# SSD stage of a hybrid backbone: two buffers for the turned tiles, and chunk products, weighted x and the chunk output's reads at later places

## The chip, the cores and the metric

The kernel runs on one core of a Trainium2 chip. The metric is the device time of one execution in microseconds. Four engines compute: TensorE (PE; its weight loads are PEld), VectorE (DVE), ScalarE (ACT) and GpSimd (POOL). SyncE (SP) issues most transfers, in the order in which they stand in its queue; a transfer that has to wait keeps those behind it waiting.

## The reference

One layer of a trunk over 256 latent tokens with 256 context tokens ahead of them. A combined input projection feeds two groups of heads, a bidirectional Mamba-2 SSD and a spatial-gating MLP, whose outputs go through one output projection. What the change touches is the SSD, cut here to what matters:

```python
def _ssd(xh, dt, A, Bm, Cm, h0, with_output):
    # x (heads' values), B and C (state space), chunks of 128 tokens
    xdt = x * dtc[..., None]
    acs = jnp.cumsum(a, axis=2)
    decay_to_end = jnp.exp(a_tot[:, :, None] - acs)
    states = jnp.einsum('bckgn,bckgr,bckgrp->bcgrpn', Bc, decay_to_end, xdt)
    ...                                     # h_starts: states carried from chunk to chunk
    CB = jnp.einsum('bcqgn,bckgn->bcgqk', Cc, Bc)
    y_diag = jnp.einsum('bcgqk,bcgrqk,bckgrp->bcqgrp', CB, Lmat, xdt)
    y_off = jnp.einsum('bcqgn,bcgrpn,bcqgr->bcqgrp', Cc, h_starts, jnp.exp(acs))
    return (y_diag + y_off).reshape(bsz, L, H, P), final
```

It runs forward and backward over the latents, starting from the context's final states, for 8 groups of 4 heads. x, B and C come from the projection through a depthwise convolution of 5 taps and SiLU.

## The kernel before

All products of the projections are in three passes with split operands: each weight tile w is split into hi (ScalarE, line 543) and lo (VectorE, line 549), and TensorE multiplies hi by hi, lo by hi and hi by lo (lines 141 to 143). The SSD stage starts after the adaLN and the first seven tiles of the projection and takes the profile's span from about 126 to 450 us. In it TensorE streams the other 25 of 32 channel tiles through (psx); each has 48 such products (16 k-steps of three), 512 or 256 columns wide.

The tiles come in groups of four: tile 4g and 4g+1 are x of group g, 4g+2 is B, 4g+3 is C. Seven tiles, among them 12, 13 and 15 of group 3, are made early and only convolved in this stage. After a tile is done, its work on the other engines is put into a queue by due times: `later(dt, fn)` files a function, `pump(dt)`, which the loop calls after every second k-step (6 products) with 1.3 (0.65 for 256 columns), advances a counter of due time and calls what is due. So a due time fixes the place of each instruction in its engine's order, and each engine works its own order off, waiting on semaphores.

For a tile: `conv_tile` sets the first tap on ScalarE (out of the accumulator psx), the other taps on VectorE (line 624, eight instructions, four for a C tile) and SiLU on ScalarE (line 627). For a group:

- x and B have to be turned (channels by tokens to tokens by channels). `by_pe` says where TensorE does it (ptx, ptb, then a ScalarE copy): group 0, and B of group 7. Elsewhere `turn` has VectorE transpose 32x32 blocks into a buffer T (tag tt: tiles tx, tb; line 739), SyncE stores T to DRAM (a tile D: Dx, Db; line 741), and `turned` reads it back by four transfers of 64 KB (xk, bk; line 747). The time allowed between both is `LAND`, 4.5.
- `ssd_w` (GpSimd) weighs x by decay for context and latents: xw in four instructions, xl in two; `ssd_sk` writes the skip term into y in two.
- `ssd_cb`, `ssd_states` (TensorE): pcb = B by C, psc = turned B by xw, psl = turned B by xl. Then `ssd_hc` (ScalarE copies psc to hs), `ssd_hd` (GpSimd decays hs), `ssd_hl` (VectorE adds psl), `ssd_o` (TensorE, pso = C by hs).
- In between, `ssd_cbm`, `ssd_mb`, `ssd_m` make M and E from pcb and the decays for both chunks, `ssd_yd` multiplies E by x (psy). `ssd_yo` and `ssd_ya` scale pso (VectorE) and add it to y (GpSimd).
- `ssd_yc` turns psy through the same path (yc, Dy), `ssd_yt` reads it back (yz), `ssd_yf` adds it to y (VectorE, line 968).
- `row_load` (GpSimd's queue, line 725) loads R, the cumulated decays of the next group, after E was taken from the one before.

The weights' raw tiles (w, 1 MB each) are loaded three ahead by SyncE, in the same queue as the turned tiles.

Of the kernel before, what the change touches and what calls it, by code (L numbers as in the profile page):

```python
# [8 lines left out]
F32 = mybir.dt.float32  # L9
# [6 lines left out]
P = 128  # L16
# [4 lines left out]
NGRP = 8  # L21
# [26 lines left out]
def tile_hybrid_ssd_mlp(  # L48
# [22 lines left out]
    def mkpool(**kw):  # L71
        return tc.tile_pool(reuse_waits="tile", **kw)
# [23 lines left out]
    y = ypool.tile([P, 2, D], F32, tag="big16", name="y")  # L96
# [48 lines left out]
    def bc(ap, axis, n):  # L145
        u = ap.unsqueeze(axis)
        shp = list(u.shape)
        shp[axis] = n
        return u.to_broadcast(shp)
# [22 lines left out]
    def spt(shape, name):  # L172
        return sps.tile(shape, F32, tag="s", name=name)
# [162 lines left out]
    for k in range(KT):  # L336
# [7 lines left out]
        g = k % 4  # L344
# [169 lines left out]
    wp["spl"] = ctx.enter_context(mkpool(name="splp", bufs=4))  # L514
    cvs = ExitStack()
    drp = ctx.enter_context(mkpool(name="drp", bufs=1, space=bass.MemoryType.DRAM))
    drt = ctx.enter_context(mkpool(name="drt", bufs=2, space=bass.MemoryType.DRAM))
    cv1 = cvs.enter_context(mkpool(name="cv1", bufs=1))
    cv2 = cvs.enter_context(mkpool(name="cv2", bufs=2))
    cv3 = cvs.enter_context(mkpool(name="cv3", bufs=3))  # L520
# [57 lines left out]
    def later(dt, fn):  # L578
        queue.append((now[0] + dt, seq[0], fn))
        seq[0] += 1  # L580
# [14 lines left out]
    def conv_tile(i, src, d0, ds):  # L595
        ch = ORDER[i]
        lat = ch >= 24
        n = 256 if lat else 512
        cw = pc[:, C_CW + 5 * i : C_CW + 5 * i + 5]
        l0 = 0 if lat else 256  # L600
        T = {}

        def tap0():
            if ch < 16:
                o = cv3.tile([P, n], F32, tag="xs", name=f"xbc{i}")
            else:
                o = cv2.tile([P, n], F32, tag="cs" if lat else "bs", name=f"xbc{i}")
            nc.scalar.activation(o, src, AF.Identity, bias=pc[:, C_CB + i : C_CB + i + 1], scale=cw[:, 2:3])  # L608
            T["o"] = o

        def taps():
            o = T["o"]
            o4 = o[:, l0 : l0 + 256].rearrange("p (r t) -> p r t", r=4)
            src4 = src[:, l0 : l0 + 256].rearrange("p (r t) -> p r t", r=4)
            for k in (0, 1, 3, 4):
                s = k - 2
                parts = [(o4, src4, 64)]
                if not lat:
                    parts.append((o[:, 0:256], src[:, 0:256], 256))
                for (a, z, w) in parts:  # L620
                    o0, o1 = max(0, -s), w - max(0, s)
                    ao = a[..., o0:o1]
                    zi = z[..., o0 + s : o1 + s]
                    nc.vector.scalar_tensor_tensor(ao, zi, cw[:, k : k + 1], ao, op0=ALU.mult, op1=ALU.add)  # L624

        def silu():
            nc.scalar.activation(T["o"], T["o"], AF.Silu)
            done[i] = T["o"]

        later(d0, tap0)  # L630
        later(d0 + 0.9, taps)
        later(d0 + ds, silu)
# [12 lines left out]
    def wctx(t, d):  # L645
        return eu[:, 4 + t if d == 0 else t]

    def wlt(d):
        return eu[:, 3 - d]
# [80 lines left out]
    gs_ = {}  # L730
# [2 lines left out]
        return ap.rearrange("p (h q) -> p h q", h=4)  # L733

    def by_pe(g, what):
        return g == 0 or g == NGRP - 1 and what != "x"

    def turn(T, src, nm):
        nc.vector.transpose(T.rearrange("p (b g c) -> p g b c", b=4, g=4), src.rearrange("p (g b c) -> p g b c", g=4, b=4))
        D = drt.tile([64, 1024], F32, tag="D", name=f"D{nm}")  # L740
        nc.sync.dma_start(D.rearrange("(b g a) (i c) -> (a i) (b g) c", b=4, g=4, c=32),
                            T.rearrange("p (u c) -> p u c", c=32))
        return D

    def turned(dst, D):
        for b in range(4):
            nc.sync.dma_start(dst[32 * b : 32 * b + 32].rearrange("p (u c) -> p u c", c=32),
                                D[16 * b : 16 * b + 16, :].rearrange("u (i c) -> i u c", c=32))

    def ssd_x(g, xi):  # L750
        S = gs_.setdefault(g, {})
        if xi == 0:
            S["xk"] = cv2.tile([P, 2, 4, P], F32, tag="xk", name=f"xk{g}")
        xt = done.pop(4 * g + xi)
        if not by_pe(g, "x"):
            T = cv1.tile([P, 512], F32, tag="tt", name=f"tx{g}{xi}")
            S["Dx", xi] = turn(T, xt, f"x{g}{xi}")
            return
        p = spt([P, 4, P], f"ptx{g}{xi}")
        for t in range(4):  # L760
            nc.tensor.transpose(p[:, t, :], xt[:, t * P : (t + 1) * P], ident)
        S["ptx", xi] = p

    def ssd_xc(g, xi):
        xk = gs_[g]["xk"][:, xi]
        if by_pe(g, "x"):
            nc.scalar.copy(xk, gs_[g]["ptx", xi])
        else:
            turned(xk.rearrange("p t c -> p (t c)"), gs_[g]["Dx", xi])

    def xtok_(g, t):
        return gs_[g]["xk"][:, :, t].rearrange("p x (h q) -> p x h q", h=2)

    def hx(ap):
        return ap.rearrange("p (x h q) -> p x h q", x=2, h=2)

    def hb(ap):
        return bc(ap.rearrange("p (x h) -> p x h", x=2), 3, 64)

    def ssd_w(g):  # L780
        S = gs_[g]
        h4 = slice(4 * g, 4 * g + 4)
        xw = cv1.tile([P, 2, 2, 256], F32, tag="xw", name=f"xw{g}")
        for t in range(2):
            for d in range(2):
                nc.gpsimd.tensor_tensor(hx(xw[:, t, d, :]), xtok_(g, t), hb(wctx(t, d)[:, h4]), op=ALU.mult)
        xl = cv1.tile([P, 2, 256], F32, tag="xl", name=f"xl{g}")
        for d in range(2):
            nc.gpsimd.tensor_tensor(hx(xl[:, d, :]), xtok_(g, 2 + d), hb(wlt(d)[:, h4]), op=ALU.mult)
        S["xw"], S["xl"] = xw, xl  # L790

    def ssd_b(g):
        bt = done[4 * g + 2]
        S = gs_.setdefault(g, {})
        S["bk"] = cv1.tile([P, 4, P], F32, tag="bk", name=f"bk{g}")
        if not by_pe(g, "b"):
            T = cv1.tile([P, 512], F32, tag="tt", name=f"tb{g}")
            S["Db"] = turn(T, bt, f"b{g}")
            return
        p = spt([P, 4, P], f"ptb{g}")  # L800
        for t in range(4):
            nc.tensor.transpose(p[:, t, :], bt[:, t * P : (t + 1) * P], ident)
        S["ptb"] = p
# [101 lines left out]
    def yg(g, c):  # L905
        return y[:, c, g * 256 : (g + 1) * 256]

    def ssd_sk(g):
        for c in range(2):
            nc.gpsimd.tensor_tensor(hx(yg(g, c)), xtok_(g, 2 + c), hb(dsk[:, 4 * g : 4 * g + 4]), op=ALU.mult)  # L910
# [59 lines left out]
    LAND = 4.5  # L970

    def plan_tile(i, src, d0=0.0, ds=5.2, tx=7.0, tw=1.5, late=0.0, td=0.0):

        g, r = divmod(i, 4)
        conv_tile(i, src, d0, ds)
        lx, lb, ly = (0.7 if by_pe(g, w) else LAND for w in "xby")
        if lx == LAND:
            tw = max(tw, 2 * LAND + 3)
        if lb == LAND:
            late = max(late, 8.0)  # L980
        if r < 2:
            later(d0 + tx, lambda: ssd_x(g, r))
            later(d0 + tx + lx, lambda: ssd_xc(g, r))
        if r == 1:
            later(d0 + tx + tw, lambda: ssd_w(g))
            later(d0 + tx + tw + 3, lambda: ssd_sk(g))
        if r == 2:
            later(d0 + tx, lambda: ssd_b(g))
            later(d0 + tx + lb, lambda: ssd_bc(g))
        if r == 3:  # L990
            d0 += late
            for t, fn in [(6, ssd_cb), (6, ssd_states), (6.9, ssd_cbm), (7.6, lambda g: ssd_mb(g, 0)), (8, ssd_hc),
                          (8.7, ssd_hd), (9.4, ssd_hl), (9.5, lambda g: ssd_m(g, 0)), (11.2, lambda g: ssd_mb(g, 1)),
                          (12, ssd_o), (12.2, lambda g: ssd_m(g, 1)), (13.9, lambda g: ssd_yo(g, 0)),
                          (14.5, lambda g: ssd_yo(g, 1)), (14.7, lambda g: ssd_ya(g, 0)), (15.3, lambda g: ssd_ya(g, 1)),
                          (16 + td, ssd_yd), (16.9 + td, ssd_yc),
                          (16.9 + td + (1.7 if ly < 1 else LAND), ssd_yt), (18.6 + td + (0.7 if ly < 1 else 2 * LAND + 2), ssd_yf)]:
                later(d0 + t, lambda fn=fn: fn(g))
            plan_d(d0 + 11, g + 1, 1.5)
            plan_e(d0 + 17, g + 1)  # L1000
# [17 lines left out]
    for n, i in enumerate(REST):  # L1018
        lat = ORDER[i] >= 24
        ps = acp.tile([P, 256 if lat else 512], F32, tag="acc", name=f"psx{i}")  # L1020
        for hf in range(2):
            whi, wlo = half(2 * n + hf)
            for kk in range(8):
                k = 8 * hf + kk
                w = slice(kk * P, (kk + 1) * P)
# [167 lines left out]
    for blk in range(16):  # L1193
# [11 lines left out]
        for u in range(8):  # L1205
            whi, wlo = half(base + blk * 8 + u)
            for kk in range(2):
                k = 2 * u + kk
                w = slice(kk * 512, (kk + 1) * 512)
# [69 lines left out]
    for i in range(8):  # L1279
        tk, b = divmod(i, 4)  # L1280
# [156 lines left out]
```

## Time and profile before

| what | us |
|---|---|
| median of 3 runs | 978.4 (976.14 to 978.86) |
| the profiled execution | 974.69 |
| its span, first to last instruction | 972.8 |
| TensorE busy in the span | 955.7 |
| VectorE busy | 685.6 |
| GpSimd busy | 198.6 |

A line of the page's groups gives the source line, engine, operation, out<-in, the count, the busy us and mean ns, and the idle time in front. A line of waits gives the engine and what it waited for, then us in total, times and the longest. In the chain of waits and the timeline the first figure is the start in us from the span's start, the second the length. A line of a stretch gives its bounds and length, then each engine's busy us with its instructions (PE, PEld, DVE, ACT, POOL), TensorE's granted clock, the share of the DMA engines and GB/s. A name ending in q is an engine's queue of issues.

### The profile page before, as it was taken

What the parts mean: (1) busy time and instruction counts of PE and PEld (TensorE: products, weight loads), DVE (VectorE), ACT (ScalarE), POOL (GpSimd) and SP (SyncE); (2) the same over time, 40 slices, a digit from 0 to 9 for tenths busy, and PEclk for the clock granted to TensorE, in tenths of its full rate; (3) what the DMA queues carried; (4) which work ended last, traced back from release to release, by engine and by line L of the source; (5) the groups of instructions that cost most, each with busy time, mean ns of one, the idle gap of its engine ahead of it and who ended that gap; (6) DMA issues with size and microseconds to landing.
All of it is one profiled execution on the core that took longest, in us unless ns stands there. A gap on an engine that the chain in (4) does not pass through costs nothing.

```text
span 972.8 us, 13786 instructions
## 1 busy us (share of the span) xinstructions
PE 955.7 (98%) x5138; PEld 771.8 (79%) x5138; DVE 685.6 (70%) x1101; ACT 482.8 (50%) x731; POOL 198.6 (20%) x290
## 2 busy tenths in 40 slices
PE   9999999998997999999999999999999999999997
PEld 4688888786785878787888888887888888888885
DVE  6888798878985868676767776767666665445636
ACT  4344458564662544455445433465565564346612
POOL 0000002522551233354000000043334541000000
PEclk9999999999999999999999999999999999999999
DMA  9999956567676666575877868686556665556722
GB/s 363 417 415 415 365 224 165 149 182 158 138 189 169 147 172 149 160 217 209 295 304 281 289 254 314 259 305 210 200 195 222 223 233 192 212 177 251 266 87 86
DMA packets 145666, 225.09 MB, mean 231 GB/s; under 512 B 114992, under 2 KB 115248, under 8 KB 122944
## 3 DMA queue, kind: packets, MB, share of 16 engines
q1 hardware_dynamic: 138816, 206.55, 62.6%
q0 software_dynamic: 6208, 16.85, 5.4%
q8 instruction: 40, 0.66, 0.3%
q10 hardware_dynamic: 576, 0.82, 0.2%
q14 instruction: 26, 0.21, 0.1%
HBM read 211.02 MB, written 8.98 MB: 226 GB/s over the span
## 4 chain that ended last, share of the span: by engine, by line
PE 87%; DMA 6%; DVE 4%; ACT 1%; SPq 1%; issue 1%; DVEq 0%; ACTq 0%
PE pa L1212 12%; PE pa L1214 12%; PE pa L1213 12%; PE psx L141 8%; PE psx L142 8%; PE psx L143 8%; PE pm L1255 3%; PE pm L1254 3%; PE pm L1253 3%; DMA ada<-in_wada_dram 3%; PE pq L1255 2%; PE pq L1254 2%; PE pq L1253 2%; PE psc L865 2%; PE pso L917 1%; DMA wst<-in_wst_dram 1%
## 5 line engine op out<-in xcount | busy, mean ns | idle before, releaser
L88 DVE TENSOR_TENSOR lo_w<-w,hi_w 128x1024 fp32r<-128x1024 f32 x173 | 210.7, 1222 | 148.8 <-ACT hi_w L87 148.7
L87 ACT CAST hi_w<-w 128x1024 fp32r<-128x1024 f32 x173 | 182.2, 1053 | 220.7 <-PE pa L1214 147.9
L1212 PE MATMUL pa<-hi_w,hhi 128*128 128x512 f32 x512 | 201.2, 393 | 0.0
L1213 PE MATMUL pa<-lo_w,hhi 128*128 128x512 f32 x512 | 199.4, 390 | 0.0
L1214 PE MATMUL pa<-hi_w,hlo 128*128 128x512 f32 x512 | 199.4, 389 | 0.0
L141 PE MATMUL psx<-hhi,hi_w 128*128 128x512 f32 (+1 forms) x400 | 151.5, 379 | 0.0
L143 PE MATMUL psx<-hhi,lo_w 128*128 128x512 f32 (+1 forms) x400 | 145.8, 364 | 0.0
L142 PE MATMUL psx<-hlo,hi_w 128*128 128x512 f32 (+1 forms) x400 | 145.7, 364 | 0.0
L1212 PEld LDWEIGHTS pa<-hi_w,hhi 128*128 128x128 f32 x512 | 96.2, 188 | 20.9 <-issue 1.6
L1214 PEld LDWEIGHTS pa<-hi_w,hlo 128*128 128x128 f32 x512 | 96.1, 188 | 20.0
L1213 PEld LDWEIGHTS pa<-lo_w,hhi 128*128 128x128 f32 x512 | 96.2, 188 | 19.8 <-issue 0.2
L624 DVE SCALAR_TENSOR_TENSOR xbc<-psx,pc,xbc 128x248 f32<-128x248 f32 (+1 forms) x204 | 83.4, 473 | 19.7 <-ACT xbc L608 19.0
L549 DVE TENSOR_TENSOR lo_w<-w,hi_w 128x1024 fp32r<-128x1024 f32 x61 | 81.8, 1349 | 20.0 <-ACT hi_w L543 20.0
L1120 POOL DMA_DIRECT2D Z<-T x128 | 73.7, 583 | 97.2 <-ACT sq L1188 33.0
L141 PEld LDWEIGHTS psx<-hhi,hi_w 128*128 128x128 f32 x400 | 75.5, 189 | 14.4 <-issue 3.1
L142 PEld LDWEIGHTS psx<-hlo,hi_w 128*128 128x128 f32 x400 | 75.6, 189 | 12.9 <-issue 1.7
L143 PEld LDWEIGHTS psx<-hhi,lo_w 128*128 128x128 f32 x400 | 75.5, 189 | 12.2
L543 ACT CAST hi_w<-w 128x1024 fp32r<-128x1024 f32 x61 | 63.6, 1045 | 42.5 <-PE psx L142 29.5
L1253 PE MATMUL pm<-hi_w,hhi 128*128 128x512 f32 x128 | 49.8, 389 | 0.0
L1255 PE MATMUL pm<-hi_w,hlo 128*128 128x512 f32 x128 | 49.8, 389 | 0.0
L1254 PE MATMUL pm<-lo_w,hhi 128*128 128x512 f32 x128 | 49.8, 389 | 0.0
L378 ACT CAST hi_st<-wst 128x448 fp32r<-128x448 f32 (+2 forms) x26 | 17.2, 679 | 57.0 <-DMA wst<-in_wst_dram 57.0
(274 smaller groups left out, 1407.6 us busy)
## 6 DMA issues: line engine op xcount, KB each, us to landing
w<-in_wlat_dram SPq DMA_DIRECT2D x64, 1024.0 KB, 4.8
w<-in_wout_dram SPq DMA_DIRECT2D x32, 1024.0 KB, 4.8
w<-in_wxbc_dram SPq DMA_DIRECT2D x25, 1024.0 KB, 5.6
ada<-in_wada_dram SPq DMA_DIRECT2D x24, 1024.0 KB, 14.0
gate<-in_wada_dram SPq DMA_DIRECT2D x16, 1024.0 KB, 5.0
ada<-in_wada_dram SPq DMA_DIRECT2D x16, 512.0 KB, 12.5
R<-acs POOLq DMA_DIRECT2D x8, 1024.0 KB, 7.0
wst<-in_wst_dram SPq DMA_DIRECT2D x15, 480.0 KB, 13.0
```

The costliest lines, as they stand in the source:

```text
L87: nc.scalar.copy(hi, raw)
L88: nc.vector.tensor_tensor(lo, raw, hi.bitcast(F32), op=ALU.subtract)
L141: nc.tensor.matmul(ps, lhsT=whi, rhs=hhi[k][:, s], start=start, stop=False)
L142: nc.tensor.matmul(ps, lhsT=whi, rhs=hlo[k][:, s], start=False, stop=False)
L143: nc.tensor.matmul(ps, lhsT=wlo, rhs=hhi[k][:, s], start=False, stop=stop)
L624: nc.vector.scalar_tensor_tensor(ao, zi, cw[:, k : k + 1], ao, op0=ALU.mult, op1=ALU.add)
L1212: nc.tensor.matmul(pa[tk], lhsT=hhi[k][:, t], rhs=whi[:, w], start=k == 0, stop=False)
L1213: nc.tensor.matmul(pa[tk], lhsT=hhi[k][:, t], rhs=wlo[:, w], start=False, stop=False)
L1214: nc.tensor.matmul(pa[tk], lhsT=hlo[k][:, t], rhs=whi[:, w], start=False, stop=k == KT - 1)
L1253: nc.tensor.matmul(p, lhsT=yh[:, t], rhs=whi[:, w], start=j == 0, stop=False)
L1254: nc.tensor.matmul(p, lhsT=yh[:, t], rhs=wlo[:, w], start=False, stop=False)
L1255: nc.tensor.matmul(p, lhsT=yl[:, t], rhs=whi[:, w], start=False, stop=hf == 0 and j == 15)
```

## The change

It has five parts. The turning buffer tt has two copies instead of one, and the DRAM tiles four instead of two. In group 7 the second x tile (tile 29) is turned by TensorE instead of VectorE and DRAM. `ssd_w` is cut in two: xl becomes `ssd_wl`, due 3 later where x is turned through DRAM, and the skip is due another 3 later. The group's products with B and all that follows them (`late`) are due 11 instead of 8 after the C tile, 14 with tile 15 (it was 10). The reads of the turned chunk output are due 3 later and their addition to y 4 later.

```diff
-    drt = ctx.enter_context(mkpool(name="drt", bufs=2, space=bass.MemoryType.DRAM))
+    drt = ctx.enter_context(mkpool(name="drt", bufs=4, space=bass.MemoryType.DRAM))
...
     def by_pe(g, what):
-        return g == 0 or g == NGRP - 1 and what != "x"
+        return g == 0 or g == NGRP - 1 and what != "x0"
...
-        if not by_pe(g, "x"):
-            T = cv1.tile([P, 512], F32, tag="tt", name=f"tx{g}{xi}")
+        if not by_pe(g, f"x{xi}"):
+            T = cv2.tile([P, 512], F32, tag="tt", name=f"tx{g}{xi}")
...
+        S["xw"] = xw
+
+    def ssd_wl(g):
+        h4 = slice(4 * g, 4 * g + 4)
         xl = cv1.tile([P, 2, 256], F32, tag="xl", name=f"xl{g}")
         for d in range(2):
             nc.gpsimd.tensor_tensor(hx(xl[:, d, :]), xtok_(g, 2 + d), hb(wlt(d)[:, h4]), op=ALU.mult)
-        S["xw"], S["xl"] = xw, xl
+        gs_[g]["xl"] = xl
...
-            T = cv1.tile([P, 512], F32, tag="tt", name=f"tb{g}")
+            T = cv2.tile([P, 512], F32, tag="tt", name=f"tb{g}")
...
-        lx, lb, ly = (0.7 if by_pe(g, w) else LAND for w in "xby")
+        lx, lb, ly = (0.7 if by_pe(g, w) else LAND for w in (f"x{r}", "b", "y"))
...
         if lb == LAND:
-            late = max(late, 8.0)
+            late = max(late, 14.0 if i == 15 else 11.0)
...
         if r == 1:
+            late_w = lx == LAND
             later(d0 + tx + tw, lambda: ssd_w(g))
-            later(d0 + tx + tw + 3, lambda: ssd_sk(g))
+            later(d0 + tx + tw + (3 if late_w else 0), lambda: ssd_wl(g))
+            later(d0 + tx + tw + (6 if late_w else 3), lambda: ssd_sk(g))
...
-                          (16.9 + td + (1.7 if ly < 1 else LAND), ssd_yt), (18.6 + td + (0.7 if ly < 1 else 2 * LAND + 2), ssd_yf)]:
+                          (16.9 + td + (1.7 if ly < 1 else LAND + 3), ssd_yt), (18.6 + td + (0.7 if ly < 1 else 2 * LAND + 6), ssd_yf)]:
```

How this moves instructions shows in three places. The first is SyncE around group 4's B: bk4 is read from Db4, which holds tb4; yz3 is the chunk output of group 3, read from Dy3; w17 and w18 are weights. Before:

```order
L747 DMA xk4_2733<-Dx41_2855 32x16x32 x4
L741 DMA Dy3_2975<-yc3_2973 128x16x32
L741 DMA Db4_3024<-tb4_3022 128x16x32
L81 DMA w17_3058<-in_wxbc_dram 128x2048
L747 DMA yz3_3032<-Dy3_2975 32x16x32 x4
L747 DMA bk4_3021<-Db4_3024 32x16x32 x4
L81 DMA w18_3150<-in_wxbc_dram 128x2048
```

Now:

```order
L747 DMA xk4_2714<-Dx41_2829 32x16x32 x4
L741 DMA Db4_3014<-tb4_3012 128x16x32
L741 DMA Dy3_3018<-yc3_3016 128x16x32
L81 DMA w17_3050<-in_wxbc_dram 128x2048
L747 DMA bk4_3011<-Db4_3014 32x16x32 x4
L747 DMA yz3_3083<-Dy3_3018 32x16x32 x4
L81 DMA w18_3134<-in_wxbc_dram 128x2048
```

B's store and reads have each changed places with the chunk output's.

The second is TensorE at group 4's products with B, among the products of tile 21; the number behind hhi and hlo is the k-step. Before:

```order
L142 MATMUL psx21_3088<-hlo5_137,hi_w28_2956 128x512
L143 MATMUL psx21_3088<-hhi5_121,lo_w28_2985 128x512
L848 MATMUL pcb4_3122<-xbc19_3004,xbc18_2896 128x128 x2
L865 MATMUL psc4_3125<-xw4_3037,bk4_3021 128x512 x2
L868 MATMUL psl4_3128<-xl4_3042,bk4_3021 128x256 x2
L141 MATMUL psx21_3088<-hhi6_122,hi_w28_2956 128x512
```

Now:

```order
L142 MATMUL psx21_3088<-hlo11_143,hi_w29_2978 128x512
L143 MATMUL psx21_3088<-hhi11_127,lo_w29_3000 128x512
L852 MATMUL pcb4_3144<-xbc19_2976,xbc18_2869 128x128 x2
L869 MATMUL psc4_3147<-xw4_3031,bk4_3011 128x512 x2
L872 MATMUL psl4_3150<-xl4_3058,bk4_3011 128x256 x2
L141 MATMUL psx21_3088<-hhi12_128,hi_w29_2978 128x512
```

They stand behind k-step 11 instead of 5, 6 k-steps or 18 products later; so do those of groups 2, 3, 5 and 6, and group 1's 6 later. Of what follows, pso and psy of groups 2, 4, 5 and 6 stand 12 products later, those of group 3 30 later.

The third is VectorE between group 5's hs and the last step of its E; the rows between are the eight taps of tile 25, of which the first and the last are shown. Before:

```order
L856 TENSOR_TENSOR cbb5_3536<-pcb5_3520,tri_ge_99 128x256
L857 TENSOR_TENSOR cbf5_3535<-pcb5_3520,tri_le_96 128x256
L549 TENSOR_TENSOR lo_w40_3562<-w20_3376,hi_w40_3550 128x1024
L887 TENSOR_TENSOR hs5_3552<-psl5_3526,hs5_3552 128x256 x2
L739 STREAM_TRANSPOSE tx60_3567<-xbc24_3494 128x4x4x32
L901 SCALAR_TENSOR_TENSOR M50_3539<-cbf5_3535,dtt_1459,M50_3539 128x128 x4
L903 TENSOR_TENSOR E5_3281<-M50_3539,E5_3281 128x512
L901 SCALAR_TENSOR_TENSOR M51_3586<-cbf5_3535,dtt_1459,M51_3586 128x128 x4
L903 TENSOR_TENSOR E5_3281<-M51_3586,E5_3281 128x512
L624 SCALAR_TENSOR_TENSOR xbc25_3614<-psx25_3487,pc_87,xbc25_3614 128x4x62
```

Now:

```order
L549 TENSOR_TENSOR lo_w40_3552<-w20_3371,hi_w40_3535 128x1024
L739 STREAM_TRANSPOSE tx60_3555<-xbc24_3494 128x4x4x32
L860 TENSOR_TENSOR cbb5_3560<-pcb5_3543,tri_ge_99 128x256
L861 TENSOR_TENSOR cbf5_3559<-pcb5_3543,tri_le_96 128x256
L891 TENSOR_TENSOR hs5_3571<-psl5_3549,hs5_3571 128x256 x2
L905 SCALAR_TENSOR_TENSOR M50_3569<-cbf5_3559,dtt_1459,M50_3569 128x128 x4
L907 TENSOR_TENSOR E5_3304<-M50_3569,E5_3304 128x512
L624 SCALAR_TENSOR_TENSOR xbc25_3595<-psx25_3487,pc_87,xbc25_3595 128x4x62
L624 SCALAR_TENSOR_TENSOR xbc25_3595<-psx25_3487,pc_87,xbc25_3595 128x254
L549 TENSOR_TENSOR lo_w41_3623<-w20_3371,hi_w41_3597 128x1024
L905 SCALAR_TENSOR_TENSOR M51_3621<-cbf5_3559,dtt_1459,M51_3621 128x128 x4
L907 TENSOR_TENSOR E5_3304<-M51_3621,E5_3304 128x512
```

The taps of tile 25 and a split (lo_w41) now stand between the two steps of M and E.

On GpSimd the order differs in group 1 alone: there xl follows M of group 0's second chunk, and the skip follows the additions to y. In groups 2 to 6 xw, xl and the skip still stand directly behind each other.

More of the change, by code (lines that the diff above doesn't have):

```diff
@@ L765, in ssd_xc @@
         xk = gs_[g]["xk"][:, xi]
-        if by_pe(g, "x"):
+        if by_pe(g, f"x{xi}"):
             nc.scalar.copy(xk, gs_[g]["ptx", xi])
```

## The prediction

> **What bounds the kernel now.** I read the page first, then TensorE's waits, then its timeline at those waits and the chain behind them. Columns of the timeline: start, us, engine, line, operation, out<-in, count, and in brackets the idle time in front with what ended it.
>
> ```profile
> span 972.8 us, 13786 instructions
> PE 955.7 (98%) x5138; PEld 771.8 (79%) x5138; DVE 685.6 (70%) x1101; ACT 482.8 (50%) x731; POOL 198.6 (20%) x290
> PE 87%; DMA 6%; DVE 4%; ACT 1%; SPq 1%; issue 1%; DVEq 0%; ACTq 0%
> ```
>
> TensorE sets the time: 17.1 us of the span are not its own. What it waits for in the SSD stage is one thing:
>
> ```profile
> PE psc L865 <- DMA bk<-Db: 8.3, 2, 5.2
> ```
>
> ```profile
> 234.69 0.60 PE L848 MATMUL pcb<-xbc,xbc 128*128 128x128 f32 x4
> 238.45 1.95 PE L865 MATMUL psc<-xw,bk 128*128 128x512 f32 x4 [3.15 <-DMA bk<-Db]
> ...
> 299.44 0.60 PE L848 MATMUL pcb<-xbc,xbc 128*128 128x128 f32 x4
> 305.21 3.43 PE L865 MATMUL psc<-xw,bk 128*128 128x512 f32 x4 [5.17 <-DMA bk<-Db]
> ```
>
> The first is group 2, the second group 4. Both times the chunk states (psc) wait for turned B. The wait has a second price: psc itself then runs slowly. The chain of waits has the undisturbed length, and two prices used below:
>
> ```profile
> 299.37 0.23 PE psx L143
> ...
> 351.41 1.72 PE psc L865 x4
> ...
> 411.12 1.02 PE psy L943 x16
> ...
> 427.67 0.44 PE ptb L802 x4
> ```
>
> So group 4 costs 5.17 + (3.43 - 1.72) = 6.88 us, group 2 costs 3.15 + (1.95 - 1.72) = 3.38 us: together 10.26 us. That is all that the change can take from TensorE.
>
> **Why B is late.** Group 2, from the chain of waits:
>
> ```profile
> 228.29 0.63 DVE tb L739
> ...
> 228.94 3.67 DMA Db<-tb
> ...
> 232.72 0.72 DVE tx L739
> ...
> 233.47 0.36 SPq L741
> ...
> 233.94 0.99 SPq L747
> ...
> 236.06 2.25 DMA bk<-Db
> ```
>
> B's store lands at 232.61, but its four reads are queued on SyncE behind the store of the next x tile, whose transpose (tx) waits until B's store has read the only turning buffer. Group 4, from the timelines of GpSimd, VectorE and SyncE:
>
> ```profile
> 288.62 2.33 POOL L786 TENSOR_TENSOR xw<-xk,ed 128x256 f32<-128x256 f32 x4
> 290.92 1.18 POOL L789 TENSOR_TENSOR xl<-xk,ed 128x256 f32<-128x256 f32 x2
> 292.06 1.17 POOL L910 TENSOR_TENSOR y<-xk,dsk 128x256 f32<-128x256 f32 x2
> ```
>
> ```profile
> 289.34 4.98 DVE L549 TENSOR_TENSOR lo_w<-w,hi_w 128x1024 fp32r<-128x1024 f32 x1
> 294.24 0.70 DVE L739 STREAM_TRANSPOSE tb<-xbc 128x512 f32<-128x512 f32 x1
> ```
>
> ```profile
> 294.97 0.38 SPq L741 DMA_DIRECT2D Db<-tb  x1
> ...
> 296.39 2.27 SPq L747 DMA_DIRECT2D yz<-Dy  x4
> 298.85 4.16 SPq L747 DMA_DIRECT2D bk<-Db  x4
> ```
>
> A weight split (lo_w, 1.23 us elsewhere, row below) takes 4.98 and ends 1.09 us after the last of eight GpSimd instructions at 293.23: it stood while they ran, 3.75 us. Then four reads of the chunk output (yz) stand ahead of B's.
>
> **The change part by part.** *Products with B later.* By the order, pcb, psc and psl stand 18 matmuls further back in groups 2 to 6 (6 in group 1). At 0.23 us each that is 18 x 0.23 = 4.1 us. Group 2 would reach psc at 235.3 + 4.1 = 239.4 instead of waiting from 235.3 to 238.45: covered by 0.95 us even with B as late as now. Group 4 needs 5.17 and gets 4.1, so 1.1 us must come from B itself.
>
> *Two turning buffers, four DRAM buffers.* tx no longer waits for B's store. Group 2's reads can go at 232.6 instead of 233.94: 1.3 us earlier, so cover 0.95 + 1.3 = 2.3 us. Nothing is added but memory.
>
> *Reads of the chunk output later.* They change places with B's reads on SyncE in group 4: 2.27 us of issue leave B's path. The stores change too: B's is now ahead of the chunk output's. The chunk products of group 3 go back by 30 matmuls (tile 15's own delay), 6.9 us, so its GpSimd work (xw of group 4 waits behind the load of R, which waits for E) moves from 288.6 to about 288.6 + 6.9 - 3.4 = 292.1, behind the split that was held and behind B's transpose. Taking out the 3.75 and the 2.27 alone makes B 6.0 us earlier against the 1.1 needed. The split that will stand beside xw now is the next one, needed some ten us later; xw and xl end near 295.6, psc starts near 299.9 + 4.1 - 3.4 = 300.6. The final add of y (yf) now stands ahead of group 4's hs add on VectorE and waits for yz; B's reads are then 6.0 - 1.1 = 4.9 us early, yz's 2.27 behind them, and hs is added over 3 us after psc's start (1.72, then the copy and GpSimd, below): zero.
>
> *GpSimd's weighted x in pieces.* By the order it changes GpSimd's sequence in group 1 alone; in groups 2 to 6 xw, xl and the skip stay neighbours and run when their x has landed. Zero, and no gap for VectorE either. [...]
>
> [...]
>
> *Group 7's second x by TensorE.* Four transposes like ptb's: +0.44 us straight on the bound. A store, four reads and a VectorE transpose (0.70) go, one ScalarE copy comes, all off the path. The transposes need the SiLU of tile 29:
>
> ```profile
> 412.11 0.63 ACT L627 ACTIVATE xbc<-xbc 128x512 f32<-128x512 f32 x1 [2.73 <-DVE xbc L624]
> ```
>
> done at 412.7; their place is 18 matmuls behind psy's old one, 412.1 + 4.1 = 416.2. No wait.
>
> *What is late next.* pso and psy move too, but by 12 matmuls in groups 2, 4, 5 and 6, so psc to pso has 24 matmuls where it had 30, 1.4 us less. VectorE's order also puts eight conv taps and a split in front of the second M. Group 5, which has no stall, gives all pieces:
>
> ```profile
> 355.17 1.05 ACT L543 CAST hi_w<-w 128x1024 fp32r<-128x1024 f32 x1 [3.52 <-PE psx L142]
> 356.13 0.58 ACT L875 COPY hs<-psc 128x512 f32<-128x512 f32 x1
> ```
>
> ```profile
> 356.78 1.75 POOL L881 TENSOR_TENSOR hs<-hs,ed 128x256 f32<-128x256 f32 x2 [3.27 <-ACT hs L875]
> ```
>
> ```profile
> 347.73 3.20 DVE L624 SCALAR_TENSOR_TENSOR xbc<-psx,pc,xbc 128x248 f32<-128x248 f32 x8 [4.17 <-ACT xbc L608]
> ...
> 356.26 1.23 DVE L549 TENSOR_TENSOR lo_w<-w,hi_w 128x1024 fp32r<-128x1024 f32 x1 [3.53 <-ACT hi_w L543]
> 357.99 0.99 DVE L887 TENSOR_TENSOR hs<-psl,hs 128x256 f32<-128x256 f32 x2 [0.51 <-POOL hs L881]
> ...
> 362.57 1.14 DVE L901 SCALAR_TENSOR_TENSOR M<-cbf,dtt,M 128x128 f32<-128x128 f32 x4 [1.22 <-POOL M L893]
> 363.75 0.69 DVE L903 TENSOR_TENSOR E<-M,E 128x512 f32<-128x512 f32 x1
> ```
>
> ```profile
> 360.64 1.88 PE L917 MATMUL pso<-hs,xbc 128*128 128x512 f32 x4
> ...
> 366.58 1.09 PE L943 MATMUL psy<-E,xk 128*64 128x128 f32 x16
> ```
>
> psc ended at 351.41 + 1.72 = 353.1 and will end at 357.2. The hs copy then no longer waits for the cast ahead of it: copy to 357.9, GpSimd 358.0 to 359.8, VectorE's hs add 359.2 to 360.2 (it overlaps GpSimd by 0.54, as now). pso moves to 360.64 + 12 x 0.23 = 363.4: margin 3.2. Then M 1.14, E 0.69, taps 3.20, split 1.23, M 1.14, E 0.69 are 8.1, to 368.3; psy moves to 366.58 + 2.8 = 369.4: margin 1.1 us. It is the thinnest, four times. I take no wait there; the ends are 0 and, if a hold of 3.75 falls into each, 4 x (3.75 - 1.1) = 10.6.
>
> **The sum.** -10.26 + 0.44 = -9.8, on the profiled span: 972.8 - 9.8 = 963.0. That execution took 974.69 in all; the runs shown have a median of 978.4 (976.14 to 978.86), so I take the difference from the median: 978.4 - 9.8 = 968.6, and leave 0.4 for thin margins: **969 us**, alone 966 to 972.
>
> **Rivals.** *Part of it comes back.* A hold of 3.75 before group 2's B (GpSimd's xw there comes earlier, as its x reads now stand ahead of yz's) makes B 3.75 - 2.3 = 1.5 late, and psy's margin of 1.1 is broken once or twice by 2.65: 1.5 to 6.8 back, 970.5 to 975.8. For it: the row of 4.98. Against, from the page's groups (busy us and mean ns behind the bar):
>
> ```profile
> L549 DVE TENSOR_TENSOR lo_w<-w,hi_w 128x1024 fp32r<-128x1024 f32 x61 | 81.8, 1349 | 20.0 <-ACT hi_w L543 20.0
> ```
>
> 61 splits at 1.349 instead of 1.23 lose 7.3 us in all, and that one row is half of it.
>
> *No gain.* VectorE is the real bound and the wait moves:
>
> ```profile
> 210.00:310.00 100.00, 91.68 (x451) 73.64 (x451) 80.58 (x146) 49.55 (x80) 37.13 (x46) 0.98 0.69 166
> ```
>
> Its busy time (third figure behind the length) is 80.6 of 100 us; ten less leave 90, so 90% and no bound by count, but if order costs it the rest, time stays at 978.
>
> *Slower.* psy waits for E in groups 2, 4, 5 and 6. Now E ends at 363.75 + 0.69 = 364.44, 2.1 us ahead of psy at 366.58. The change takes 1.4 us of distance and puts 4.4 us (taps 3.20, split 1.23) in between. If nothing before them moves up, each group loses 1.4 + 4.4 - 2.1 = 3.7: 4 x 3.7 = 14.8 against 9.8, so 978.4 + 5.0 = 983.4. It decides from 9.8 / 4 = 2.5 us a group. Against it: the hs copy no longer loses 3.0 us behind the cast and M no longer 1.22 for GpSimd, which is the sum above.
>
> *The change does not do what it says* holds for the GpSimd pieces, at no price.
>
> **How the numbers follow.** Forecast 0.62, partly back 0.20, no gain 0.11, slower 0.07. 0.3% is 2.9 us, about what a measurement here can tell from no change. Faster: the forecast and nine tenths of the second, 0.80; within: the third and the rest of the second, 0.13; slower 0.07. The range goes from 964 (runs differ by 2.7 among themselves) to 977, which holds the first two cases and leaves out most of the others.
>
> **What would show it.** Right: no row of psc waiting for bk; psc at 1.72 in all groups; in group 4 B's reads ahead of yz's; tx directly behind tb. Wrong: a TensorE wait for DVE hs (pso) or DVE E (psy), for xw, or for lo_w; splits over 3 us beside xw; a span above 970.

## The result, and the profile after

The changed kernel takes 968.83 us (median of 6 runs, 968.41 to 973.45) against 977.23 for the kernel before in the same comparison (976.14 to 978.86). The ratio is 0.9922, 95% interval 0.9901 to 0.9943: faster by 0.6 to 1.0%. Run once more beside later experiments it came to 970.59 against 974.8, 0.9943 (0.9927 to 0.9959). The forecast was 969, with 964 to 977 as its range.

The page of the changed kernel, its span, engines and chain of waits:

```profile
span 967.1 us, 13788 instructions
PE 955.2 (99%) x5142; PEld 771.1 (80%) x5142; DVE 683.8 (71%) x1100; ACT 481.5 (50%) x732; POOL 192.4 (20%) x290
PE 72%; DMA 12%; DVE 9%; issue 3%; ACT 2%; SPq 1%; POOL 1%; DVEq 0%; ACTq 0%; POOLq 0%
```

The span fell by 5.7 us in the two profiled executions; the medians fell by 8.4 in this comparison and by 4.2 in the later one. TensorE's own work is what it was (955.7 and 955.2); what shrank is the rest of the span. The chain names more DMA and VectorE than before; I take it that with TensorE at 99% several chains end close together, which no run singles out. TensorE's waits in the changed kernel (first line) and its timeline at the two places:

```profile
PE psc L869 <- DMA bk<-Db: 3.1, 2, 1.6
```

```profile
238.45 0.60 PE L852 MATMUL pcb<-xbc,xbc 128*128 128x128 f32 x4
240.71 1.96 PE L869 MATMUL psc<-xw,bk 128*128 128x512 f32 x4 [1.65 <-DMA bk<-Db]
...
301.73 0.60 PE L852 MATMUL pcb<-xbc,xbc 128*128 128x128 f32 x4
303.82 1.95 PE L869 MATMUL psc<-xw,bk 128*128 128x512 f32 x4 [1.49 <-DMA bk<-Db]
```

The same two waits for turned B are still there, shorter: 8.3 us became 3.1, and group 4's psc runs in 1.95 instead of 3.43. That is 5.2 + 1.5, less 0.44 for group 7's transposes: 6.3 of gain, of which 5.7 arrived in the span. The forecast had no wait left. So B did not come as early as the sum supposed. SyncE's timeline around group 2's and group 4's B:

```profile
231.15 0.38 SPq L741 DMA_DIRECT2D Db<-tb  x1
231.74 0.73 SPq L741 DMA_DIRECT2D Dx<-tx  x1
232.56 1.38 SPq L81 DMA_DIRECT2D w<-in_wxbc_dram  x1
234.23 2.26 SPq L747 DMA_DIRECT2D bk<-Db  x4
...
290.17 0.38 SPq L741 DMA_DIRECT2D Db<-tb  x1
290.76 0.74 SPq L741 DMA_DIRECT2D Dy<-yc  x1
291.55 1.40 SPq L81 DMA_DIRECT2D w<-in_wxbc_dram  x1
293.25 6.08 SPq L747 DMA_DIRECT2D bk<-Db  x4
299.44 4.46 SPq L747 DMA_DIRECT2D yz<-Dy  x4
```

Two things stand out. In group 2 the first read goes at 234.23, no earlier than before (233.94). In group 4 it goes at 293.25, 5.6 us earlier than before (298.85) and ahead of the chunk output's, as forecast; but the issue of the four takes 6.08 instead of 4.16. And in both places a weight load of 1 MB (L81) now stands directly ahead of B's reads. The chain of waits shows what the reads of group 4 then cost:

```profile
294.16 4.00 SPq L747
...
298.20 5.48 DMA bk<-Db
```

One issue stands for 4.00 us and the last read takes 5.48 to land (2.56 before). The time from issue to landing of all four reads of group 2, first the kernel before, then the changed one:

```profile
DMA to landing us min/median/max: 2.3/2.6/2.9
```

```profile
DMA to landing us min/median/max: 4.6/5.3/5.5
```

### The profile page after: what moved, and what is told of

Read it like the earlier page. It is cut to its first block, busy times and chain, and to the rows that moved or that the text cites. A ratio compares the mean times of both kernels' runs of the same rounds, so it can differ in the third digit from the quotient of the medians.

```text
span 967.1 us, 13788 instructions
## 1 busy us (share of the span) xinstructions
PE 955.2 (99%) x5142; PEld 771.1 (80%) x5142; DVE 683.8 (71%) x1100; ACT 481.5 (50%) x732; POOL 192.4 (20%) x290
## 4 chain that ended last, share of the span: by engine, by line
PE 72%; DMA 12%; DVE 9%; issue 3%; ACT 2%; SPq 1%; POOL 1%; DVEq 0%; ACTq 0%; POOLq 0%
PE pa L1218 8%; PE pa L1220 8%; PE pa L1219 8%; PE psx L141 8%; PE psx L142 7%; PE psx L143 7%; DMA ada<-in_wada_dram 4%; DMA gate<-in_wada_dram 4%; PE pm L1261 3%; PE pm L1259 3%; PE pm L1260 3%; DVE lo_w L88 2%; PE pq L1261 2%; PE pq L1260 2%; PE pq L1259 2%
## 5 line engine op out<-in xcount | busy, mean ns | idle before, releaser
L88 DVE TENSOR_TENSOR lo_w<-w,hi_w 128x1024 fp32r<-128x1024 f32 x173 | 210.0, 1222 | 136.6 <-ACT hi_w L87 136.4
L549 DVE TENSOR_TENSOR lo_w<-w,hi_w 128x1024 fp32r<-128x1024 f32 x61 | 77.4, 1276 | 19.1 <-ACT hi_w L543 19.1
L1072 DVE SCALAR_TENSOR_TENSOR junk<-gate,cb 128x2048 bf16<-128x2048 f32 x16 | 36.7, 2291 | 18.2 <-DMA gate<-in_wada_dram 18.1
```

The lines of the kernel that those rows point to most:

```text
L88: nc.vector.tensor_tensor(lo, raw, hi.bitcast(F32), op=ALU.subtract)
```

## The experiments

**1. The later products alone** (the kernel before with this edit):

```diff
-            late = max(late, 8.0)
+            late = max(late, 14.0 if i == 15 else 11.0)
```

> The kernel before with one part of the change: the products with B and what follows due 11 (14 with tile 15) instead of 8 (10). Theory (the place of the products carries the gain): 966 to 971, TensorE's waits for B at most 3.1 us in all, as in the changed kernel. Rival (two turning buffers and the later reads make B earlier and carry part of it): with one buffer B's reads of group 2 stay behind the store of the next x tile, the waits for B stay above 3.1 us, 972 to 976.

973.58 us against 975.7, ratio 0.9977 (0.9966 to 0.9988): a quarter to a half of the change. TensorE's waits in the SSD stage and, from VectorE's timeline, the row behind them:

```profile
PE pso L917 <- ACT R L817: 3.2, 1, 3.2
PE psx L141 <- DVE xbc L624: 1.7, 2, 1.2
PE psc L865 <- DMA bk<-Db: 1.4, 1, 1.4
PE psy L943 <- DVE E L903: 0.6, 1, 0.6
```

```profile
235.49 0.71 DVE L739 STREAM_TRANSPOSE tx<-xbc 128x512 f32<-128x512 f32 x1 [3.29 <-DMA Db<-tb]
...
251.62 0.71 DVE L887 TENSOR_TENSOR hs<-psl,hs 128x256 f32<-128x256 f32 x2
```

The time lies in the rival's range, but neither theory had these waits. The wait for B is down to 1.4, yet waits for VectorE appear instead. The one for pso is put down to ScalarE's R; but pso began at 252.48, just behind VectorE's hs add (251.62 + 0.71 = 252.33), so I read it as a wait for hs. VectorE is late because the next x tile's transpose has to wait 3.29 us until B's store has read the only turning buffer, and everything in VectorE's queue stands behind it.

**2. The two turning buffers alone** (cv2 for tag tt, four DRAM tiles).

```diff
-    drt = ctx.enter_context(mkpool(name="drt", bufs=2, space=bass.MemoryType.DRAM))
+    drt = ctx.enter_context(mkpool(name="drt", bufs=4, space=bass.MemoryType.DRAM))
...
-            T = cv1.tile([P, 512], F32, tag="tt", name=f"tx{g}{xi}")
+            T = cv2.tile([P, 512], F32, tag="tt", name=f"tx{g}{xi}")
...
-            T = cv1.tile([P, 512], F32, tag="tt", name=f"tb{g}")
+            T = cv2.tile([P, 512], F32, tag="tt", name=f"tb{g}")
```

> The kernel before with only the two turning buffers and the four DRAM tiles. Theory of the prediction: B's reads of group 2 go 1.3 us earlier, its wait falls from 3.15 to about 1.9, group 4 stays at 5.2: some 1.3 us off, 975 to 977. Rival: in SyncE's order the load of w13 (1 MB), which stood ahead of the x tile's store, now stands directly ahead of B's reads, so these land later: group 2 waits 3.15 us or longer, 977 or above.

975.77 against 975.7, ratio 0.9997 (0.9985 to 1.0009): nothing. SyncE's timeline in group 2, and the landing of the four reads there:

```profile
230.62 0.84 SPq L81 DMA_DIRECT2D w<-in_wxbc_dram  x1
231.60 2.12 SPq L747 DMA_DIRECT2D bk<-Db  x4
```

```profile
DMA to landing us min/median/max: 4.6/5.1/5.4
```

The reads go 2.3 us earlier (231.60 against 233.94), more than the 1.3 of the prediction, and land as late: psc starts at 237.90 instead of 238.45 after a wait of 3.07. The time lies in the range of the prediction's theory; the reads speak for the rival: the x tile's store, which no longer waits, now stands ahead of w13, and the 1 MB comes to stand directly ahead of the reads. The four DRAM tiles were not tried apart from the second buffer.

**3. Small loads of w13 and w17.** The changed kernel, with 128 of the 2048 columns of these two weights loaded, and used for all (the cast and the split are changed to read them over and over; these lines are not shown):

```diff
-        nc.sync.dma_start(raw, src)
+        if name in ('w13', 'w17'):
+            nc.sync.dma_start(raw[:, 0:128], src[:, 0:128])
+        else:
+            nc.sync.dma_start(raw, src)
```

> The changed kernel with the loads of the weights w13 and w17, which stand directly ahead of B's reads of groups 2 and 4, cut from 1 MB to 64 KB: of each only 128 of its 2048 columns are loaded and used sixteen times over, so the products of those two tiles are not the reference's; instructions and order are the same. Theory (the 1 MB ahead in the same queue makes B's reads slow): the last read of group 4 lands 2.3 to 3.5 us after its issue instead of 5.48, TensorE's waits for B (3.1 us) are gone, 965 to 966. Rival (the reads are slow for GpSimd's load of R, or late for VectorE's sake): waits of 1.4 to 1.7 us stay, 968 to 969.

968.69 us, ratio 0.9926 (0.9909 to 0.9944): the time of the changed kernel. The landing of group 2's reads, then of group 4's, and TensorE's waits:

```profile
DMA to landing us min/median/max: 2.1/2.3/2.3
...
DMA to landing us min/median/max: 5.5/6.1/6.5
```

```profile
PE pso L931 <- DVE hs L901: 1.2, 1, 1.2
PE psx L144 <- DVE xbc L634: 1.2, 1, 1.2
PE psy L957 <- DVE E L917: 0.2, 1, 0.2
```

The cause of the slow reads is settled for group 2: without the 1 MB ahead they land in 2.3 us instead of 5.3. In group 4 the longest falls from 9.8 to 6.5 only; GpSimd's load of R, another 1 MB, is issued at 292.21 in the changed kernel, just ahead of the reads, and took 10.5 us to land there, 5.1 before. That it accounts for the rest was not tried, but experiment 4 fits: there R's load is issued behind the four reads (293.08), and they land in 2.3 to 4.9. Both waits for B are gone, as the theory said, and the time is not: of the 3.1 us, 2.6 come back as waits for VectorE, at hs in group 2, then at E and the taps behind group 4's products (psx for xbc; I read it as the accumulator that the taps have yet to read). VectorE stands about a microsecond behind B. Ahead of the hs add of group 2 four taps of an early tile take 3.15 us there, while GpSimd makes M and decays hs; four such taps took 1.65 in the kernel before (at 234.47).

**4. Products another 18 later** (the changed kernel with 14 and 17 in place of 11 and 14).

```diff
-            late = max(late, 14.0 if i == 15 else 11.0)
+            late = max(late, 17.0 if i == 15 else 14.0)
```

> The changed kernel with the products due another 3 later (14, and 17 with tile 15), some 18 products or 4.1 us. Theory (what is left is 1.65 and 1.49 us of waiting for B, and nothing behind them is near its limit): no wait for B, 965 to 966. Rival (the margins of E ahead of psy and of the hs add ahead of pso are used up, or xw is late now): TensorE waits for E, hs or xw, 968 to 974.

964.52 us against 975.7, ratio 0.9885 (0.987 to 0.9901), span 962.8: the theory's number was 965 to 966. TensorE's waits over the whole span begin with

```profile
PE px L1361 <- ACT dg L1360: 1.5, 1, 1.5
PE psw L323 <- DVE ones L111: 1.1, 1, 1.1
```

and neither is in the SSD stage, where none is left. This removes B and VectorE at once: pso and psy move back too, and so VectorE's deadlines. It also moves the reads: B's store of group 4 goes at 284.48 instead of 290.17, and group 2's reads now stand ahead of w13, with w12 3 us ahead of them.

**5. Later products and two buffers together**, without the other three parts (the edits of 1 and 2).

> The kernel before with two parts of the change together, the later products (due 11, and 14 with tile 15) and the two turning buffers; not the later reads of the chunk output, the pieces on GpSimd and group 7's x by TensorE. Theory (each of the two is worth little alone, 2.1 and 0 us, since with one buffer the next x transpose holds VectorE while B's store reads it, and with the early products TensorE waits anyway; together they are the change): 968 to 970.5, like the changed kernel, no wait of TensorE for hs or E over 1 us. Rival (the later reads or the pieces carry a part too): 971.5 to 974.

969.86 us against 974.8, ratio 0.9941 (0.9927 to 0.9955). The changed kernel in the same comparison:

> The changed kernel itself, unaltered, beside the others on one chip: 967.5 to 970.5.

970.59, ratio 0.9943 (0.9927 to 0.9959). So, as far as these runs can tell, these two parts are the change; alone they gave 2.1 and 0 us, together 4.9. Its waits in the stage are others, though. They sum to 5.0 us, against 3.1 to 3.5 for B in the changed kernel, which has 0.44 of transposes more; a difference of about a microsecond that the times don't show:

```profile
PE psc L865 <- DMA bk<-Db: 2.4, 2, 1.4
PE psx L141 <- DVE xbc L624: 1.7, 2, 1.2
PE psy L943 <- DVE E L903: 0.9, 1, 0.9
```

**6. The changed kernel with one buffer** (the edit of 2 taken back).

> The changed kernel with one turning buffer and two DRAM tiles again. Theory (the next x transpose holds VectorE for some 3 us behind B's store in group 2, and what VectorE owes TensorE comes late): waits for hs, E or the taps of 3 to 6 us in all, 972 to 975. Rival (the second buffer does nothing, as it did alone): 968 to 970.

972.35, ratio 0.9974 (0.9962 to 0.9985), the gain of the later products alone. VectorE's stall and what it does to TensorE, in a profiled execution that is the longest of the twelve (976.38; the others took 971.95 to 974.04):

```profile
234.97 0.71 DVE L739 STREAM_TRANSPOSE tx<-xbc 128x512 f32<-128x512 f32 x1 [3.88 <-DMA Db<-tb]
```

```profile
PE pso L921 <- DVE hs L891: 3.6, 1, 3.6
PE psc L869 <- DMA bk<-Db: 3.5, 2, 1.9
```

A stall of 3.88 us on VectorE at 231 is a wait of 3.60 for TensorE at 249. In the kernel before, the same stall (2.8 us) is followed by no wait of TensorE for VectorE; it waited for B there anyway.

**7. The two parts with the products at 14 and 17** (the edits of 2 and 4 on the kernel before).

> The kernel before with two turning buffers and the products due 14 (17 with tile 15), and nothing else of the change. Theory (these two are all that is needed): TensorE without a wait over 0.5 us in the SSD stage, 963.5 to 965.5, or some 0.4 less than the changed kernel with the products as late, since group 7's second x stays off TensorE. Rival (the later reads of the chunk output or the pieces keep VectorE or GpSimd ahead): 966 to 970.

964.96 us against 974.8, ratio 0.9894 (0.9876 to 0.9912), span 962.3, no wait in the stage. It is 5.6 us below the changed kernel of the same comparison, with four lines edited. Against the kernel of experiment 4 the difference is less than can be told.

**8. The other three parts, each taken back from the changed kernel.** The reads of the chunk output and their addition to y:

```diff
-  (16.9 + td + (1.7 if ly < 1 else LAND + 3), ssd_yt), (18.6 + td + (0.7 if ly < 1 else 2 * LAND + 6), ssd_yf)]:
+  (16.9 + td + (1.7 if ly < 1 else LAND), ssd_yt), (18.6 + td + (0.7 if ly < 1 else 2 * LAND + 2), ssd_yf)]:
```

> The changed kernel with the reads of the turned chunk output and their addition to y due as before (3 and 4 earlier). Theory (with the products later, SyncE already reads group 4's B ahead of the chunk output, so this part moves nothing that TensorE waits for): like the changed kernel, 968 to 971. Rival (the addition to y, earlier on VectorE, holds the taps until yz has landed): waits of TensorE for xbc or E of 1 to 3 us, 971 to 973.

GpSimd's pieces (`ssd_wl` due with `ssd_w`, the skip 3 later):

```diff
-            later(d0 + tx + tw + (3 if late_w else 0), lambda: ssd_wl(g))
-            later(d0 + tx + tw + (6 if late_w else 3), lambda: ssd_sk(g))
+            later(d0 + tx + tw + 0, lambda: ssd_wl(g))
+            later(d0 + tx + tw + 3, lambda: ssd_sk(g))
```

> The changed kernel with GpSimd's xl and skip due as before, at once behind xw. Theory (the order of GpSimd differs in group 1 alone, and nothing waits there): like the changed kernel, 968 to 971, the same waits for B. Rival (the pieces keep VectorE's splits out of a hold): splits over 3 us, 971 or more.

Group 7's second x back to DRAM (its pieces on GpSimd together, else xl would stand behind the products that read it):

```diff
-        return g == 0 or g == NGRP - 1 and what != "x0"
+        return g == 0 or g == NGRP - 1 and what[0] != "x"
```

> The changed kernel with group 7's second x turned by VectorE and DRAM as before (and its pieces on GpSimd together). Theory: four transposes fewer on TensorE, 0.44 us less: 967.5 to 970.5, not to be told from the changed kernel. Rival (x by DRAM comes late for group 7's products): a wait for xw or xk, over 971.

970.33, 968.76 and 967.54 us against 976.3: ratios 0.994 (0.9927 to 0.9953), 0.9929 (0.9916 to 0.9942) and 0.9921 (0.9905 to 0.9937). All three intervals overlap with the changed kernel's; none of the three parts has an effect that these runs can tell. For the reads the profile tells more. TensorE's waits, and SyncE's order in group 4, without that part:

```profile
PE psc L869 <- DMA bk<-Db: 2.1, 2, 1.2
PE psx L141 <- DVE xbc L624: 1.2, 1, 1.2
PE psy L947 <- DVE E L907: 0.9, 1, 0.9
```

```profile
296.05 4.93 SPq L747 DMA_DIRECT2D bk<-Db  x4
301.43 1.89 SPq L747 DMA_DIRECT2D yz<-Dy  x4
```

B's reads stand ahead of the chunk output's without it: the later products did that. What the part does is to trade: 2.1 us of waits for VectorE go, 1.0 to 1.4 of waits for B come. With the pieces undone no split came in sight of a hold either; the waits for B are 2.9 us, with 0.5 for the taps.

**9. Later still** (two buffers, products at 17 and 20).

> The kernel before with two turning buffers and the products due 17 (20 with tile 15), another 18 products behind the kernel that had 14 (17) and no wait left. Theory (no wait is left to be taken, and the slack behind the products is not yet used up): as with 14 (17), 964 to 966. Rival (now what follows the products is late: hs for pso, E for psy, or the next group's buffers): waits of 2 us or more, 967 to 972.

968.33 against 976.3, ratio 0.9924 (0.9908 to 0.994): more than half of what the step to 14 and 17 had added is lost again (0.9941 in experiment 5, 0.9894 in 7), and the rival's mechanism is seen:

```profile
PE psy L943 <- DVE E L903: 1.7, 1, 1.7
PE ptb L802 <- ACT xbc L627: 1.2, 1, 1.2
```

Its waits are under the 2 us that were expected, and they make 2.9 of the 4.7 us by which its span exceeds that of experiment 7 (967.0 and 962.3). Most of the rest is clock: about a microsecond after the first of these waits eight products take 3.4 us instead of 1.8, at a granted clock of 0.57 between 291 and 295. So, of the three places tried, 14 is better than 11 and 17.

## Why the prediction was right, and where not

**What bounds the kernel, and the most it can give: right.** The prediction put all that can be taken from TensorE at 10.26 us. Experiments 4 and 7, with no wait left in the stage, have spans 10.0 and 10.5 below the 972.8 of before. The term for slow products is a little too large: the undisturbed 1.72 is a row of the chain of waits, 3.43 and 1.95 are rows of the timeline, and there the undisturbed four take 1.88 (group 5, 351.24). By the timeline alone the sum is 9.94.

**The products' move: right in size, wrong in cover.** TensorE reached group 2's pcb at 238.45 instead of 234.69, close to the 4.1. The step that failed is "covered by 0.95 us even with B as late as now". B was later than then, for two reasons: its transpose came at 230.2 to 230.9 in the kernels with the products at 11 (228.2 and 227.8 in those without), and with two buffers its reads took 4.0 to 5.5 us. VectorE's order ahead of that transpose is the same; one row of it has become longer. VectorE and GpSimd in the kernel before, then in the changed one:

```profile
220.53 3.22 DVE L624 SCALAR_TENSOR_TENSOR xbc<-y,pc,xbc 128x248 f32<-128x248 f32 x8
...
225.44 3.32 POOL L786 TENSOR_TENSOR xw<-xk,ed 128x256 f32<-128x256 f32 x4 [11.17 <-PE psx L143]
```

```profile
220.21 6.09 DVE L624 SCALAR_TENSOR_TENSOR xbc<-y,pc,xbc 128x248 f32<-128x248 f32 x8
...
219.84 3.17 POOL L786 TENSOR_TENSOR xw<-xk,ed 128x256 f32<-128x256 f32 x4 [6.12 <-DMA yz<-Dy]
```

Eight taps of an early tile take 2.9 us longer while GpSimd works on xw, xl and the skip of group 2 (219.84 to 226.0). GpSimd is 5.6 us earlier, and the reads of x now stand ahead of the chunk output's on SyncE (213.55; 220.59 before). All nine profiles with the products at 11 have these taps at 6.08 or 6.09, experiment 1 too, so the later products alone bring it; the five others have them at 3.22. With the products at 14 the taps end at 222.7, just as GpSimd starts, and B's store goes at 227.8 again. That GpSimd is the cause is read from these rows; no run moves it alone. This is close to what the rival "part of it comes back" named: GpSimd's xw earlier, something held ahead of group 2's B, B 1.5 late (the wait was 1.65). It looked for the hold at a split, and it is at the taps. It takes both reasons to make the wait: with quick reads it is gone (experiment 3), and in experiment 2, with slow reads but an early transpose, psc could start at 237.90, ahead of 239.06, where the changed kernel's TensorE begins to wait (an estimate from these two rows).

**Two turning buffers: the mechanism was mis-placed.** The term was 1.3 us of cover through B's earlier reads. The reads did go earlier, by 2.3 in experiment 2, and gained nothing, because the same edit put 1 MB ahead of them. What the buffers are worth is VectorE: 3.3 to 3.9 us of stall, which the prediction did not price since in the trace of before it hid behind TensorE's wait. It is uncovered by the very part that shortens that wait. This is why the parts don't add: 2.1 alone and 0 alone, 4.9 together.

**"B 6.0 us earlier" in group 4: right for the issue, wrong for the landing.** The first read went 5.6 us earlier; the last landed 1.4 earlier (303.68 against 302.52 + 2.56 = 305.08). The step took transfers' durations from the old place. In the new one w17 and R's load ran at the same time. The term was credited to the later chunk reads; experiment 8 shows that the later products make that exchange by themselves. The hold of 3.75 us at the split is gone, as said: xw went at 292.82 (forecast 292.1), and no split took over 2 us beside it; the hold that came is the one at group 2's taps.

**Pieces on GpSimd and group 7's x: as forecast**, nothing, and too little to be told.

**The margins behind: right for pso and psy, but not complete.** No wait for E or hs in the changed kernel. The thin margin of 1.1 us for psy is real in group 4, one of its four groups: without the later chunk reads (experiment 5 and the first of 8) TensorE waits 0.9 for E there. The 1.7 of experiment 9 is in group 3, which the prediction did not list. Not named was the wait of a tile's products for the taps of an earlier one (psx for xbc, 1.2 us in experiments 1, 3, 5 and in the first of 8).

**The rivals.** "Partly back" had the mechanism of group 2's wait, as shown above; the medians, 968.83 and 970.59, lie below and at the lower end of its 970.5 to 975.8. "No gain, VectorE is the real bound" is half true: in the changed kernel it is B that is late, but experiment 3 shows VectorE as the next limit about a microsecond behind. Of the signs that the prediction named, "no row of psc waiting for bk" did not come; tx does stand directly behind tb, B's reads ahead of yz's, and none of the signs of being wrong is in the changed kernel's first profile. "Slower" did not come: the hs copy and the add moved up as the sum said.

**The number.** The sum on the span was 963.0 and the span is 967.1: 4.1 us too little, 3.1 of them the waits for B that stayed; the rest was not found. The forecast of 969 fits the median all the same, since the base of 978.4, from three runs, was high: the kernel before had medians of 974.8 to 977.2 in this and the later comparisons. Against a base of 976 the same working would have given 967. So the number was met partly by luck: a gain put too large and a base too high offset each other. The base varies with the clock: in the three later comparisons the kernel before took 973.7 to 975.0 in its 18 executions with a mean granted clock of 0.997, and 977.2 to 979.0 in its seven with 0.992 or 0.993. The profiled one (974.69, 0.997) is of the short kind, so the 10.26 is the price of the waits in a cheap execution. Without waits in the stage (experiments 4 and 7) nine of ten executions had 0.998 or more and took 964.1 to 965.0.

## What to carry to other kernels

A stall that hides behind another has a price only once the other is gone, so parts of a change have to be priced together, and with each one's cover named after the others are applied. When a read is moved earlier in a queue, take its duration from what will then stand ahead of it and beside it, not from the old place (group 2's four reads landed within 2.3 to 2.9 us in the old place, 4.6 to 5.5 in the new); look where the large loads end up. When an engine's work moves, look at what then runs beside it: GpSimd's pieces of group 2, earlier by 5.6 us, met eight taps of VectorE that took 6.09 us instead of 3.22, ahead of the very tile that was to come earlier. When a wait shrinks, ask how far behind the next engine is (here 1 us), and try one more step of the same kind before refining: moving the products twice as far, with two buffers, gave more than the whole change, and three times as far lost more than half of that step again.

## What the runs showed of the hardware

**Small reads behind a large load in one queue.** Four reads of 64 KB landed 2.3 to 2.9 us after issue in group 2 of the kernel before, where 1 MB was issued 4.5 us ahead of them, 4.0 to 5.5 in the seven profiles with 1 MB issued directly ahead, within 1.7 us, 2.1 to 2.3 with that load cut to 64 KB (experiment 3). The prediction had priced the reads by how they landed in their old place.

**After a short wait of TensorE, products can be slow.** The rows are from TensorE's timeline: one buffer (experiment 6), where the first is group 2 and the second group 4; the later products alone (experiment 1), group 2; then the changed kernel run again, group 4:

```profile
252.50 1.95 PE L921 MATMUL pso<-hs,xbc 128*128 128x512 f32 x4 [3.60 <-DVE hs L891]
...
307.97 3.19 PE L869 MATMUL psc<-xw,bk 128*128 128x512 f32 x4 [1.92 <-DMA bk<-Db]
```

```profile
252.48 3.37 PE L917 MATMUL pso<-hs,xbc 128*128 128x512 f32 x4 [3.22 <-ACT R L817]
```

```profile
304.22 2.73 PE L869 MATMUL psc<-xw,bk 128*128 128x512 f32 x4 [2.21 <-DMA bk<-Db]
```

Four products of one shape take 1.95 us after a wait of 3.60 (1.88 undisturbed), 3.37 after one of 3.22 at the same place, and 3.19 after one of 1.92; the granted clock of experiment 6 was 1.00 around the first row (250 to 256) and 0.86 around the second (300 to 312), and that of the last row 0.83 in the ten microseconds around it. At group 2's psc a wait of 3.15 was followed by 1.95 in the kernel before (clock 1.00 from 230 to 242), and one of 3.07 by 2.74 in experiment 2. In the changed kernel's first profile a wait of 1.49 in group 4 cost nothing more (1.95, clock 1.00 from 300 to 310); one of 1.66 in experiment 9 was followed by eight products at about half pace (3.4 us instead of 1.8, clock 0.57). So what a wait costs beyond itself cannot be read off its length; what decides it, no run shows.
